# A four-layer hybrid model on one core: the first norm from the input's rows, inputs tile by tile, no weight part on GpSimd at the start, a shorter last norm, and unread products wherever TensorE's work thins out

## The chip, the cores and the metric

One core of a Trainium2 chip runs the whole kernel in one launch. The metric is the device time of that launch in microseconds. The engines are named as in the profile: PE (TensorE; PEld is its weight load), DVE (VectorE), ACT (ScalarE), POOL (GpSimd) and SP (SyncE, which issues most DMAs).

## The reference, cut to what matters

One sequence of 512 tokens, width 1024, float32, goes through four layers. Each has a token mixer and a SwiGLU feed-forward block of 2816 hidden columns, each ahead of it a norm, each added back to the residual. The mixers are, in turn, RWKV-7 (a recurrence with 16 heads of 64), attention over a window of 128 with a sink, a spatial gating unit and gated linear attention.

```python
def rmsnorm(x, g):
    xf = x.astype(jnp.float32)
    y = xf * lax.rsqrt(jnp.mean(jnp.square(xf), -1, keepdims=True) + NORM_EPS)
    return (y * g).astype(x.dtype)

# for each layer i:
#   x = x + mixer_i(rmsnorm(x, norm_mix[i]))
#   x = x + swiglu(rmsnorm(x, norm_ffn[i]), ffn_w_in[i], ffn_w_out[i])
# out = rmsnorm(x, norm_final)
```

## The kernel before

**Arithmetic.** A float32 operand is split into a high part (`whi`, a rounding on ACT) and a low part (`wlo`, a subtraction on DVE), both of a fast matmul type, and a product is made of three: high by high, high by low, low by high (`mm3`). `weights` loads a tile of 128x1024 (`wraw`) with a DMA from SP and splits it; with `pool` set, POOL does the subtraction. The feed-forward blocks make the products of a 2x2 blocking with seven multiplications in place of eight.

**Order.** The program isn't issued as it is written. Every operation is recorded with its dependences and a price (`price`), and `run` then issues one instruction at a time: of those that are free, the one that can start first by a model of the engines' times, which `now` keeps. So the order on each engine follows modelled times, not measured ones. All engine instructions leave from one line of `record`, and have that line in the profile: L233. Groups are therefore told apart by the names of their tiles.

**Unread products.** Before `run` issues a PE instruction that by the model starts at `s`, `keep_warm` looks at the gap since PE's last: if it is at least `GAP` = 450 ns, it is filled with products of a 128x128 identity by itself, into a PSUM bank that nobody reads. They are recorded as `ps<-ident` from L448. `count` adds up the columns that PE works off in each `TICK` of 3413 ns of the model, from which `run` guesses whether the clock is up.

**The start.** The residual lies in eight tiles `h` of 128 features x 512 tokens. They are loaded from `x_t`, the input with its axes exchanged. ACT squares the eight tiles, DVE adds them (7 additions), PE turns the sum (4 transposes, `ps<-ident,slot`) so that a reduction gives the mean square of each token (`ms`), `rsqrt` takes nine small steps to the reciprocal root (`rcol`), PE spreads it over the partitions (4 transposes, `ps<-ident,rcol`), DVE copies that out of the bank (`slot<-ps`), and the tiles are scaled one by one. Then comes the first product, of the mixer's key projection: eight steps `k`, each with a weight tile `rw_w_k` and 24 products `ps<-slot,whi` and `ps<-slot,wlo`.

**The first mixer** ends with the recurrence. Per group of heads it inverts triangular 64x64 blocks (`mt`, `iv`, `pr`, with copies between PE, DVE and ACT at each step), and then runs a chain over the chunks: `ps<-st,ident` and `ps<-st,qk` wait for the state, `ps<-vu,tok` for a copy by ACT. The out-projection is `ps<-et,rk`.

**The second mixer**, attention, makes scores for the heads of a group (`ps<-slot` of 128x256), exponentials and sums on ACT and DVE, and scaled rows on POOL; then PE turns the probabilities (`ps<-ident,slot`) and multiplies. Projections that don't depend on them (`ps<-whi,slot`, `ps<-wlo,slot`) may lie between.

**The last norm.** `finish` gathers the squares of each half of a row block and multiplies it by the norm's row `g` as it becomes ready; `store` scales each half (the left on DVE, the right on ACT) into a new tile, and sends out eight tiles of 128x512.

## Time and profile before

| | us |
|---|---|
| three timed runs, median (lowest to highest) | 2604.38 (2601.57 to 2606.51) |
| profiled execution, time | 2596.65 |
| its span | 2595.0 |
| its mean granted clock of PE | 0.994 |
| busy: PE, DVE, ACT, POOL | 2517.9, 1802.4, 1314.1, 377.6 |

Times in the views are microseconds from the start of the span. A row of a timeline gives the start, the length, the engine, the line, the operation, its output and inputs by their names, the shapes and the count of records, and in brackets the idle time ahead of it and what ended that. A row of a group gives the busy time, the mean of one record in ns, and the idle time of the engine ahead of such instructions with what ended most of it. Some float32 instructions of PE leave two records each; the unread products do.

### The profile page before, as it was taken

Reading aid. Unit: us, or ns where it says so; the run is one execution under the profiler, and the core shown is the slowest. Engines: PE = TensorE matmul, PEld = TensorE weight load, DVE = VectorE, ACT = ScalarE, POOL = GpSimd, SP = SyncE. Lnnn points to the kernel's source line nnn. Section 1 sums busy time; section 2 is a strip of 40 time slices with the busy share of each in tenths; the row PEclk is TensorE's granted clock in tenths of the full one; section 3 lists DMA queues with packets and bytes.
Section 4 is the critical chain, followed back from the end, with each engine's and each line's share of the span. In section 5 each row is a group of like instructions: output and inputs, shape, how many; then the busy total and the mean of one; then the engine's idle time right before and its main releaser. Section 6 shows DMA issues by size and latency. Waiting matters only on the chain.

```text
span 2595.0 us, 37573 instructions
## 1 busy us (share of the span) xinstructions
PE 2517.9 (97%) x14378; PEld 2052.6 (79%) x14378; DVE 1802.4 (69%) x2804; ACT 1314.1 (51%) x2156; POOL 377.6 (15%) x521
## 2 busy tenths in 40 slices
PE   9999898999999989999999999999999999999998
PEld 8577777997888756988787888888878777888886
DVE  8685875487778863787776655577868634577868
ACT  4544454465646455656464333565556523565555
POOL 1000111022112232121221000012111000121111
PEclk9999999999999999999999999999999999999999
DMA  3220001489898412898985232389887221489885
GB/s 128 62 75 10 10 4 59 120 195 225 214 225 176 129 49 49 179 211 225 213 218 146 90 98 83 82 216 228 208 213 187 84 81 57 98 219 226 221 199 117
DMA packets 126004, 365.20 MB, mean 141 GB/s; under 512 B 13296, under 2 KB 19952, under 8 KB 125824
## 3 DMA queue, kind: packets, MB, share of 16 engines
q0 software_dynamic: 41472, 138.43, 29.8%
q1 hardware_dynamic: 84352, 224.37, 26.9%
q8 instruction: 113, 1.85, 0.3%
q14 instruction: 67, 0.55, 0.1%
HBM read 358.29 MB, written 2.10 MB: 139 GB/s over the span
## 4 chain that ended last, share of the span: by engine, by line
PE 47%; DMA 5%; issue 5%; DVE 4%; ACT 3%; POOL 0%; SPq 0%; ACTq 0%; POOLq 0%; DVEq 0%
PE ps L233 47%; DMA wraw<-ffn_w_b 3%; DVE slot L233 2%; ACT slot L233 2%; DMA wraw<-ffn_o_a 2%; DVE wlo L233 1%; ACT whi L233 1%; DMA wraw<-ffn_w_a 1%; DVE h L233 0%; POOL wraw L233 0%; DVE mx L233 0%; DMA slot<-slot 0%; SPq L233 0%; DVE left L233 0%; ACT left L233 0%
## 5 line engine op out<-in xcount | busy, mean ns | idle before, releaser
L233 PE MATMUL ps<-whi,slot 128*128 128x512 f32 (+1 forms) x5072 | 1557.7, 384 | 17.8 <-DVE slot L233 9.3
L233 PEld LDWEIGHTS ps<-whi,slot 128*128 128x128 f32 x5072 | 943.7, 188 | 199.5 <-issue 21.4
L233 DVE TENSOR_TENSOR wlo<-wraw,whi 128x1024 fp32r<-128x1024 f32 (+2 forms) x628 | 720.2, 1153 | 398.8 <-ACT whi L233 396.4
L233 ACT CAST whi<-wraw 128x1024 fp32r<-128x1024 f32 (+3 forms) x632 | 625.1, 993 | 732.2 <-PE ps L233 554.7
L233 PE MATMUL ps<-wlo,slot 128*128 128x512 f32 (+1 forms) x2536 | 969.1, 383 | 1.9 <-DVE wlo L233 1.7
L233 PEld LDWEIGHTS ps<-wlo,slot 128*128 128x128 f32 x2536 | 476.9, 188 | 86.1 <-DVE wlo L233 6.2
L233 PE MATMUL ps<-slot,whi 128*128 128x512 f32 (+2 forms) x864 | 275.8, 397 | 0.1
L233 DVE TENSOR_TENSOR slot<-ps,slot 128x512 f32<-128x512 f32 (+2 forms) x287 | 155.0, 566 | 91.0 <-PE ps L233 61.7
L233 PEld LDWEIGHTS ps<-slot,whi 128*128 128x128 f32 (+2 forms) x864 | 157.2, 185 | 48.3 <-issue 6.6
L233 POOL DMA_DIRECT2D wraw<-ffn_w_a x128 | 109.1, 853 | 512.5 <-DVE wlo L233 375.7
L233 PE MATMUL ps<-slot,wlo 128*128 128x512 f32 (+2 forms) x432 | 169.5, 393 | 0.8 <-DVE wlo L233 0.8
L233 POOL DMA_DIRECT2D wraw<-ffn_w_b x64 | 54.7, 859 | 772.7 <-DMA wraw<-ffn_w_b 517.8
L233 DVE TENSOR_TENSOR slot<-left,slot 128x512 fp32r<-128x512 f32 (+1 forms) x214 | 137.5, 661 | 34.3 <-ACT slot L233 28.8
L233 DVE TENSOR_TENSOR h<-h,ps 128x512 f32<-128x512 f32 x192 | 127.1, 683 | 29.8 <-PE ps L233 28.4
L233 ACT CAST slot<-left 128x512 fp32r<-128x512 f32 (+1 forms) x214 | 123.8, 598 | 34.3 <-PE ps L233 26.4
L233 PEld LDWEIGHTS ps<-ident,slot 128*128 128x128 f32 (+1 forms) x676 | 69.2, 141 | 41.9 <-POOL slot L233 14.4
L233 ACT COPY slot<-ps 128x512 f32<-128x512 f32 (+1 forms) x137 | 75.2, 563 | 50.8 <-PE ps L233 49.2
L233 PE MATMUL ps<-ident,slot 128*128 128x128 f32 (+1 forms) x676 | 89.4, 268 | 11.4 <-POOL slot L233 9.0
L233 PEld LDWEIGHTS ps<-slot,wlo 128*128 128x128 f32 (+2 forms) x432 | 79.6, 184 | 21.3 <-issue 3.3
L233 POOL DMA_DIRECT2D wraw<-ffn_o_a x64 | 54.5, 852 | 278.6 <-DVE wlo L233 204.9
L233 ACT COPY left<-ps 128x512 f32<-128x512 f32 x100 | 50.5, 555 | 54.7 <-PE ps L233 54.7
L233 DVE TENSOR_TENSOR slot<-slot 128x512 fp32r<-128x512 f32 (+9 forms) x93 | 62.0, 672 | 15.8 <-ACT slot L233 14.6
(278 smaller groups left out, 2267.3 us busy)
## 6 DMA issues: line engine op xcount, KB each, us to landing
wraw<-ffn_w_a SPq DMA_DIRECT2D x128, 512.0 KB, 6.5
wraw<-ffn_w_a POOLq DMA_DIRECT2D x128, 512.0 KB, 6.1
wraw<-ffn_o_a SPq DMA_DIRECT2D x64, 512.0 KB, 5.0
wraw<-ffn_o_a POOLq DMA_DIRECT2D x64, 512.0 KB, 8.0
wraw<-ffn_w_b SPq DMA_DIRECT2D x64, 384.0 KB, 3.3
wraw<-ffn_w_b POOLq DMA_DIRECT2D x64, 384.0 KB, 6.2
wraw<-ffn_o_b SPq DMA_DIRECT2D x16, 512.0 KB, 4.3
wraw<-ffn_o_b POOLq DMA_DIRECT2D x16, 512.0 KB, 7.7
```

The source lines that it names most:

```text
L233: op = self.add(eng.name, lambda: getattr(eng.target, what)(*map(real, args), **{k: real(a) for k, a in kw.items()}), *self.price(eng.name ...
```

## The change

Four things, and all of them through the same recorder:

1. **First norm.** `token_squares` loads the input's rows `x` as eight tiles of 128 tokens x 512; six are squared with their sums on ACT, the last two go through DVE's statistics instructions, and the mean square of each token is there without a transpose. The tiles of `x_t` are loaded one by one within the loop over `k`, between the weight tiles. ACT, not DVE, copies the spread root out of the bank, and step `k` = 0 reads the bank itself (`near`).
2. **No weight part on POOL.** The first four subtractions of `rw_w_k` go to DVE like the others.
3. **Last norm.** The left half isn't multiplied by `g` ahead of time; `store` does that and the scaling in one instruction, both halves are scaled in place, and 4 transfers of 128x1024 take the place of 8.
4. **A guard.** `ahead_of_cold`: before a PE instruction is issued, the columns in the last `TICK` up to that instruction's modelled end are summed (`recent`). If they have once reached `DENSE` = 3500 and would now fall below it, an unread product goes ahead, and all is looked at again. It works for gaps of any length, shorter than `GAP` too.

```diff
@@ -194,7 +194,7 @@
     WINDOW, SLACK, SEM = 700, 200.0, 100.0
     FREE, GAP, TAIL, TURN = 4, 450.0, 150.0, 92.0
-    TICK, BUSY = 10240 / 3, 3350.0
+    TICK, BUSY, DENSE = 10240 / 3, 3350.0, 3500.0
     def __init__(self, tc):
         self.tc, self.ops, self.last = tc, [], None
@@ -202,6 +202,7 @@
         self.tensor, self.vector, self.scalar = Engine(self, "PE", nc.tensor), Engine(self, "DVE", nc.vector), Engine(self, "ACT", nc.scalar)
         self.gpsimd, self.sync = Engine(self, "POOL", nc.gpsimd), Engine(self, "SP", nc.sync)
         self.cold, self.warm, self.fills, self.form = 0.0, None, 0, (P, P, 0)
+        self.recent, self.armed = [], False
     def pool(self, name, bufs, **kw):
         return Pool(self, name, bufs, kw)
@@ -344,7 +345,7 @@
             s, i, op, e = best
             if e == "PE" and self.warm and op.ready > 0.0:
                 now["PE"] = self.keep_warm(now["PE"], s, work)
-                if now["PE"] > s:
+                if now["PE"] > s or self.ahead_of_cold(now, s, op, work):
                     continue
             avail[e].remove((i, op))
             if op.table and op.table != table and not (table and op.table in ALSO.get(table, ())):
@@ -412,7 +413,36 @@
             t += c
             now = t
+    def ahead_of_cold(self, now, s, op, work):
+        pool, call, first = self.warm
+        free = pool.slots["ps"].free
+        t, end = max(s, now["PE"]), s + op.cost
+        if not first.done or not free or min(free) + self.SEM > t:
+            return False
+        sum_ = op.columns
+        for b, e, c in reversed(self.recent):
+            if e <= end - self.TICK:
+                break
+            sum_ += c * (e - max(b, end - self.TICK)) / (e - b)
+        if sum_ >= self.DENSE:
+            self.armed = True
+            return False
+        if not self.armed:
+            return False
+        cost = 224.0 if work.get(int(t // self.TICK) - 1, 0.0) >= self.BUSY else 448.0
+        call()
+        self.fills += 1
+        self.form = P, P, 0
+        self.count(work, self.TICK, t, cost, 512.0)
+        now["PE"] = t + cost
+        return True
     def count(self, work, span, t, cost, columns):
+        self.recent.append((t, t + cost, columns))
+        if len(self.recent) > 400:
+            del self.recent[:200]
         n = int(t // span)
         part = min(1.0, ((n + 1) * span - t) / cost)
         work[n] = work.get(n, 0.0) + columns * part
@@ -598,8 +624,9 @@
             sq = self.slot()
             nc.scalar.activation(sq, self.h[b][:, c], AF.Square, accum_out=self.ss[:, 2 * b + nh:2 * b + nh + 1])
         if self.kind == 'final':
-            for b in bs:
-                nc.vector.tensor_mul(self.h[b][:, c], self.h[b][:, c], self.g[nh])
+            if nh:
+                for b in bs:
+                    nc.vector.tensor_mul(self.h[b][:, c], self.h[b][:, c], self.g[nh])
             return
         t = slice(half * 256, half * 256 + 256)
         for u in range(2):
@@ -673,25 +700,47 @@
         self.rsqrt(col, ms)
         return col
-    def rstd(self, acc=None):
+    def token_squares(self):
         nc = self.nc
-        if acc is None:
+        ss, ms = self.sm.tile([P, 2 * NB], F32, name="ss2"), self.sm.tile([P, NB], F32, name="ms")
+        st, mv = self.lay.tile([P, 2, 6], F32, name="xst"), self.lay.tile([P, 2], F32, name="xmv")
+        for j in range(2):
+            for b in range(NB):
+                x = self.slot()
+                nc.sync.dma_start(x, self.d['x'][b * P:(b + 1) * P, j * S:(j + 1) * S])
+                if b == NB - 1:
+                    nc.vector.bn_stats(st[:, j, :], x)
+                else:
+                    nc.scalar.activation(x, x, AF.Square, accum_out=ss[:, 2 * b + j:2 * b + j + 1])
+        nc.vector.bn_aggr(mv, st)
+        s2 = ss.rearrange("p (b n) -> p b n", b=NB)
+        l = NB - 1
+        nc.vector.scalar_tensor_tensor(ms[:, l:], mv[:, 0:1], mv[:, 0:1], mv[:, 1:2], op0=ALU.mult, op1=ALU.add)
+        nc.vector.tensor_scalar(ms[:, l:], ms[:, l:], EPS, None, op0=ALU.add)
+        nc.vector.tensor_add(ms[:, :l], s2[:, :l, 0], s2[:, :l, 1])
+        nc.vector.tensor_scalar(ms[:, :l], ms[:, :l], 1.0 / D, EPS, op0=ALU.mult, op1=ALU.add)
+        return ms
+    def rstd(self, ms=None):
+        nc = self.nc
+        if ms is None:
             col = self.rcol()
         else:
-            ms, col = [self.sm.tile([P, NB], F32, name=n) for n in ("ms", "rcol")]
-            ps = self.bank()
-            for b in range(NB):
-                nc.tensor.transpose(ps[:, b * P:(b + 1) * P], acc[:, b * P:(b + 1) * P], self.ident)
-            nc.vector.tensor_reduce(ms, self.blocks(ps), axis=AX.X, op=ALU.add)
-            nc.vector.tensor_scalar(ms, ms, 1.0 / D, EPS, op0=ALU.mult, op1=ALU.add)
+            col = self.sm.tile([P, NB], F32, name="rcol")
             self.rsqrt(col, ms)
         ps = self.bank()
         for b in range(NB):
             nc.tensor.transpose(ps[:, b * P:(b + 1) * P], col[:, b:b + 1].to_broadcast([P, P]), self.ident)
         bc = self.slot()
-        nc.vector.tensor_copy(bc, ps)
-        return col, bc
+        if ms is None:
+            nc.vector.tensor_copy(bc, ps)
+            return col, bc
+        nc.scalar.copy(bc, ps)
+        return ps, bc
     def operand(self):
         self.op = self.nx
@@ -933,18 +982,14 @@
         xq, tp = self.pool("xq", 8, tall), self.pool("tp", 3, tall)
         hn = self.h
+        ms = self.token_squares()
+        v = self.v = self.load_cols()
         nc.vector.memset(keep, 1.0)
         nc.vector.memset(self.blocks(keep, S // 64)[:, :, 0:1], 0.0)
         nc.vector.memset(sel, 0.0)
         nc.vector.memset(sel[:64, 14:15], 1.0)
         nc.vector.memset(sel[64:, 15:16], 1.0)
-        acc = self.slot()
-        for k in range(KT):
-            t = acc if k == 0 else tp.tile([P, S], F32, name="t")
-            nc.scalar.activation(t, hn[k], AF.Square)
-            if k:
-                nc.vector.tensor_add(acc, acc, t)
-        _, rbc = self.rstd(acc=acc)
+        near, rbc = self.rstd(ms)
         xx = []
         def mixed(c, k):
@@ -964,12 +1009,13 @@
         rf, kf = [[keepers.tile([P, S], F32, name="rk") for _ in range(KT)] for _ in range(2)]
         ps = [self.bank() for _ in range(KT)]
         for k in range(KT):
-            nc.vector.scalar_tensor_tensor(hn[k], hn[k], g(k), rbc, op0=ALU.mult, op1=ALU.mult)
+            nc.sync.dma_start(hn[k], d['x_t'][k * P:(k + 1) * P, :])
+            nc.vector.scalar_tensor_tensor(hn[k], hn[k], g(k), rbc if k else near, op0=ALU.mult, op1=ALU.mult)
             b = xq.tile([P, S], F32, name="xx")
             nc.vector.tensor_sub(b[:, 1:], hn[k][:, :S - 1], hn[k][:, 1:])
             nc.vector.tensor_scalar(b[:, 0:1], hn[k][:, 0:1], -1.0, None, op0=ALU.mult)
             xx.append(b)
-            hi, lo = self.weights(d['rw_w_k'][k * P:(k + 1) * P, :], 1, D, k < 4)
+            hi, lo = self.weights(d['rw_w_k'][k * P:(k + 1) * P, :], 1, D)
             x = mixed(2, k)
             for n in range(KT):
                 c = slice(n * P, (n + 1) * P)
@@ -1668,14 +1714,10 @@
             col = self.rcol(half * 2, half * 2 + 2)
             for j in range(2):
                 b = half * 2 + j
-                for nh in range(2):
-                    c = slice(nh * S, nh * S + S)
-                    o = self.slot()
-                    if nh:
-                        nc.scalar.activation(o, self.h[b][:, c], AF.Identity, scale=col[:, j:j + 1])
-                    else:
-                        nc.vector.tensor_scalar(o, self.h[b][:, c], col[:, j:j + 1], None, op0=ALU.mult)
-                    nc.sync.dma_start(self.d['out'][b * P:(b + 1) * P, c], o)
+                l, r = self.h[b][:, :S], self.h[b][:, S:]
+                nc.vector.scalar_tensor_tensor(l, l, col[:, j:j + 1], self.g[0], op0=ALU.mult, op1=ALU.mult)
+                nc.scalar.activation(r, r, AF.Identity, scale=col[:, j:j + 1])
+                nc.sync.dma_start(self.d['out'][b * P:(b + 1) * P, :], self.h[b])
 def consts():
@@ -1769,8 +1811,6 @@
 def trace(prog, d, es, stages):
     k = K(prog, d, es)
     k.h = k.eight()
-    k.load_x(k.h)
-    k.v = k.load_cols()
     g_mix = lambda i: (lambda j: k.v['norm_mix'](i * KT + j))
     g_ffn = lambda i: (lambda j: k.v['norm_ffn'](i * KT + j))
     for n, st in enumerate(stages):
```

Engine instructions now have L234, the unread products L478. By kind there are 262 unread products, 190 before: 67 up to the first product that counts (78 before), 164 from there to the end of the first mixer (90), 11 in attention (none), and 20 elsewhere (22).

**The start, on PE.** Before, the sum of squares is turned (`ps<-ident,slot`) between two runs of unread products:

```order
L448 MATMUL ps<-ident 128x128 x30
L233 MATMUL ps<-ident,vraw 128x128 x2
L448 MATMUL ps<-ident 128x128 x6
L233 MATMUL ps<-ident,slot 128x128 x4
L448 MATMUL ps<-ident 128x128 x19
L233 MATMUL ps<-ident,rcol 128x128 x4
L448 MATMUL ps<-ident 128x128 x23
L233 MATMUL ps<-slot,whi 128x512 x6
```

Now, up to the same first product:

```order
L478 MATMUL ps<-ident 128x128 x30
L234 MATMUL ps<-ident,vraw 128x128 x2
L478 MATMUL ps<-ident 128x128 x20
L234 MATMUL ps<-ident,rcol 128x128 x4
L478 MATMUL ps<-ident 128x128 x17
L234 MATMUL ps<-slot,whi 128x512 x8
```

The transposes of the sum are gone, and 37 unread products stand where 48 stood. On SP eight tiles of `x`, the two of `vecs` and then `x_t` and `rw_w_k` in turn take the place of eight tiles of `x_t`, `vecs` and five of `rw_w_k`. On DVE the first `wlo` stands ahead of the last step to `rcol`.

**The last inverse of the first mixer, on PE.** Its steps wait for copies of each other's results. Before, other groups' work lies between them, and no unread product:

```order
L233 MATMUL ps<-wu,iv 64x64 x5
L233 MATMUL ps<-mt 64x64 x16
L233 MATMUL ps<-wu,iv 64x64 x7
L233 MATMUL ps<-ident,mt 64x64 x16
L233 MATMUL ps<-vu,pr 64x64 x3
L233 MATMUL ps<-mt,pr 64x64 x16
L233 MATMUL ps<-vu,pr 64x64
L233 MATMUL ps<-wu,iv 64x64 x2
L233 MATMUL ps<-mt 64x64 x16
L233 MATMUL ps<-wu,iv 64x64
L233 MATMUL ps<-iv,mt 64x64 x24
```

Now:

```order
L478 MATMUL ps<-ident 128x128 x2
L234 MATMUL ps<-mt 64x64 x16
L478 MATMUL ps<-ident 128x128 x4
L234 MATMUL ps<-ident,mt 64x64 x16
L478 MATMUL ps<-ident 128x128 x3
L234 MATMUL ps<-mt,pr 64x64 x16
L478 MATMUL ps<-ident 128x128 x4
L234 MATMUL ps<-mt 64x64 x16
L234 MATMUL ps<-iv,mt 64x64 x7
L478 MATMUL ps<-ident 128x128 x4
L234 MATMUL ps<-iv,mt 64x64 x9
```

Unread products stand ahead of the same steps, and the chain's products (`wu,iv`, `vu,pr`) come after them. Behind this, in the last chain, 33 products of the out-projection `ps<-et,rk` stand between the chain's steps, where before 1 did.

**Attention, second group of heads, on PE.** `ps<-slot` are the scores, `whi` and `wlo` the out-projection of the group before, and `ps<-ident,slot` the first transposes of the probabilities. Before:

```order
L233 MATMUL ps<-slot 128x256 x9
L233 MATMUL ps<-whi,slot 128x512
L233 MATMUL ps<-wlo,slot 128x512
L233 MATMUL ps<-whi,slot 128x512 x2
L233 MATMUL ps<-wlo,slot 128x512
L233 MATMUL ps<-whi,slot 128x512 x2
L233 MATMUL ps<-wlo,slot 128x512
L233 MATMUL ps<-ident,slot 128x128 x2
L233 MATMUL ps<-whi,slot 128x512
```

Now the last rows of a run that is three times as long:

```order
L234 MATMUL ps<-whi,slot 128x512 x2
L234 MATMUL ps<-wlo,slot 128x512
L234 MATMUL ps<-whi,slot 128x512 x2
L234 MATMUL ps<-wlo,slot 128x512
L234 MATMUL ps<-whi,slot 128x512
L478 MATMUL ps<-ident 128x128 x3
L234 MATMUL ps<-ident,slot 128x128 x2
L234 MATMUL ps<-whi,slot 128x512
```

Between the scores and the transposes there are 24 products of the out-projection and 3 unread ones (8 and none before). In the first group of heads there are 33 for 11 at the same place. What moves ahead is missing from a later run. In the scores of each group stand 4 unread products. From the second feed-forward block on PE's order is that of before, up to two unread products in the tail that are gone.

More of the change, by code (lines that the diff above doesn't have):

```diff
@@ L940, in rwkv @@
         nc.vector.memset(sel[64:, 15:16], 1.0)
-        acc = self.slot()
-        for k in range(KT):
-            t = acc if k == 0 else tp.tile([P, S], F32, name="t")
-            nc.scalar.activation(t, hn[k], AF.Square)
-            if k:
-                nc.vector.tensor_add(acc, acc, t)
-        _, rbc = self.rstd(acc=acc)
+        near, rbc = self.rstd(ms)
         xx = []
```

4 lines of the change are left out of this document (1 added, 3 removed).

## The prediction

> **What bounds the kernel now.** I read the busy times of the engines first, then the chain of work that ended last, and then a table of busy time by stage.
>
> ```profile
> PE 2517.9 (97%) x14378; PEld 2052.6 (79%) x14378; DVE 1802.4 (69%) x2804; ACT 1314.1 (51%) x2156; POOL 377.6 (15%) x521
> PE 47%; DMA 5%; issue 5%; DVE 4%; ACT 3%; POOL 0%; SPq 0%; ACTq 0%; POOLq 0%; DVEq 0%
> ```
>
> TensorE is busy for 2517.9 us of 2595.0, so all idle time together is 77 us, and an edit can gain only in the stages where PE waits or where its clock is down. The table by stage says where these are (columns: length, then busy time and instructions of PE, its weight loads, DVE, ACT and POOL, the granted clock, the DMA share and GB/s).
>
> ```profile
> 0.00:24.36 24.36, 20.90 (x167) 20.58 (x167) 16.02 (x37) 9.04 (x12) 5.36 (x8) 1.00 0.60 205
> 24.36:195.00 170.64, 167.03 (x796) 119.64 (x796) 133.83 (x222) 82.41 (x123) 6.93 (x13) 1.00 0.23 71
> 195.00:480.00 285.00, 263.94 (x3625) 219.79 (x3620) 185.53 (x386) 127.80 (x271) 43.56 (x147) 0.99 0.08 24
> 480.00:890.00 410.00, 405.21 (x2011) 343.12 (x2010) 315.63 (x436) 229.85 (x343) 82.45 (x87) 1.00 0.80 190
> 890.00:1005.00 115.00, 101.19 (x449) 60.55 (x448) 68.52 (x159) 62.70 (x209) 39.06 (x37) 0.96 0.23 66
> 1005.00:2575.00 1570.00, 1551.62 (x7314) 1282.92 (x7313) 1069.72 (x1527) 795.72 (x1186) 200.22 (x229) 1.00 0.67 162
> 2575.00:2595.00 20.00, 8.05 (x36) 5.95 (x34) 13.13 (x41) 6.61 (x13) 0.00 (x0) 0.78 0.28 105
> ```
>
> Four stages have something to win: the first 24.36 us, in which PE does nothing but unread products; the recurrence of the first mixer (195 to 480), with 285.00 − 263.94 = 21.1 us idle; the attention of the second (890 to 1005), with 13.8 us idle at a clock of 0.96; and the last 20 us. The order of the instructions is the same in both kernels from the second feed-forward block to the tail, and there I change nothing.
>
> **The start.** The timeline from the first unread product to the first product that counts:
>
> ```profile
> 1.43 8.96 PE L448 MATMUL ps<-ident 128*128 128x128 f32 x60 [1.43 <-POOL ident L233]
> 7.42 2.67 ACT L233 ACTIVATE t<-h 128x512 f32<-128x512 f32 x4 [0.52 <-DMA h<-x_t]
> 10.22 0.38 PE L233 MATMUL ps<-ident,vraw 128*128 128x128 f32 x2
> 12.23 4.67 POOL L233 TENSOR_TENSOR wlo<-wraw,whi 128x1024 fp32r<-128x1024 f32 x2 [10.86 <-ACT whi L233]
> 13.04 0.69 DVE L233 TENSOR_REDUCE ms<-ps 128x4 f32<-128x512 f32 x1 [0.81 <-PE ps L233]
> 17.16 0.17 DVE L233 SCALAR_TENSOR_TENSOR rs_t<-ms,rs_t 128x4 f32<-128x4 f32 x1
> 17.36 0.16 DVE L233 SCALAR_TENSOR_TENSOR rcol<-rs_t,rcol 128x4 f32<-128x4 f32 x1
> 18.84 0.62 PE L233 MATMUL ps<-ident,rcol 128*128 128x128 f32 x4 [1.60 <-DVE rcol L233]
> 19.30 5.30 PE L448 MATMUL ps<-ident 128*128 128x128 f32 x46
> 19.50 0.69 DVE L233 COPY slot<-ps 128x512 f32<-128x512 f32 x1 [0.81 <-PE ps L233]
> 24.36 1.76 PE L233 MATMUL ps<-slot,whi 128*128 128x512 f32 x6
> L233 DVE TENSOR_TENSOR wlo<-wraw,whi 128x1024 fp32r<-128x1024 f32 (+2 forms) x628 | 720.2, 1153 | 398.8 <-ACT whi L233 396.4
> ```
>
> An unread product leaves two records, so 46 records are 23 products and one costs 5.30 / 23 = 0.23 us. On PE's side the new start is 30 products to 10.4, the two transposes of the vectors to 10.6, 20 products × 0.23 = 4.6 to 15.2, the transposes of rcol 0.62 to 15.8, and 17 × 0.23 = 3.9 to 19.7. On the data's side: the eight tiles of x stand first on SP, as those of x_t did, so the last square can begin about where a fifth tile's would, 7.42 + 3 × 0.67 = 9.4, and the last tile's statistics (one 128x512 pass of DVE, 0.69) end near 10.8. Then DVE has some 16 small steps at 17.36 − 17.16 = 0.2 us, 3.2 us, and one subtraction of a weight's low part, which now stands ahead of the last step of rcol: 1.15. That gives 15.2, so both sides meet at rcol near 15.2 to 15.8. From the transposes of rcol to the first product there were 24.36 − 18.84 = 5.5 us, of which the copy of 0.69 goes, since the first tile is scaled straight from the bank: 4.8. The first product comes at about 20.2, 4.2 us earlier. If the vectors, the first x_t and the first weight, which now stand behind 2 MB of x on SP, come late, rcol is held behind that subtraction and as little as 2 us is left; if the model's order binds at 19.7, it is 4.7. I take **−4.2**.
>
> The four subtractions that leave POOL took 4.67 / 2 = 2.33 us each there and take 1.15 on DVE, 4.6 us of new DVE work between the first product and the fifth tile. They lie beside 24 products per tile, of 0.23 us each: 5.5 us of PE per tile against some 4.2 of DVE (the subtraction, and four passes of 0.69 to 0.9). While that cover holds they cost nothing; without it, 4 × 1.15 = 4.6. One wait for a low part goes with them, of 0.78:
>
> ```profile
> 47.81 0.50 PE L233 MATMUL ps<-slot,wlo 128*128 128x512 f32 x1 [0.78 <-DVE wlo L233]
> ```
>
> With it the start is worth **−5** (−1 to −6).
>
> **The recurrence of the first mixer.** Here the guard puts in most: the count of unread products from 24 us to the end of this mixer goes from 90 to 164, 74 more. The groups of PE instructions that wait, and the row of the unread ones:
>
> ```profile
> L233 PE MATMUL ps<-vu,tok 128*128 128x128 f32 x112 | 20.5, 305 | 4.5 <-ACT vu L233 4.3
> L233 PE MATMUL ps<-et,rk 128*128 128x256 f32 x156 | 19.2, 282 | 0.0
> L448 PE MATMUL ps<-ident 128*128 128x128 f32 x126 | 16.9, 281 | 0.0
> L233 PE MATMUL ps<-st,ident 128*128 128x128 f32 x96 | 16.7, 296 | 3.7 <-DVE st L233 3.6
> L233 PE MATMUL ps<-ident,mt 64*64 64x64 f32 x384 | 14.6, 229 | 3.9 <-DVE mt L233 3.8
> L233 PE MATMUL ps<-mt 64*64 64x64 f32 x384 | 13.8, 221 | 1.6 <-DVE mt L233 1.5
> L233 PE MATMUL ps<-mt,pr 64*64 64x64 f32 x256 | 9.2, 221 | 0.7 <-ACT mt L233 0.7
> L233 PE MATMUL ps<-iv,mt 64*64 64x64 f32 x192 | 7.9, 227 | 1.4 <-DVE iv L233 1.4
> ```
>
> One product costs 16.9 / 63 = 0.27 us here, so 74 are 19.9 us of PE. They cost nothing as far as they lie in waits: ahead of the inverse's steps there are 3.9 + 1.6 + 0.7 + 1.4 = 7.6 us of waits, and I let 2.4 more fall into the chain's; that hides 10 and leaves **+10** on the path. (All hidden: 0. None: +19.9.) Against that, 33 products of the out-projection, ps<-et,rk at 19.2 / 156 = 0.123 us, 4.1 us together, move from behind the last chain into its waits, of which there are 4.5 + 3.7 in all: **−3.5** (0 to −4.1). And the guard is to keep the clock up in that chain:
>
> ```profile
> 447.33 0.71 PE L233 MATMUL ps<-vu,tok 128*128 128x128 f32 x4 [1.45 <-ACT vu L233]
> 449.00:453.00 4.00, 3.82 (x19) 3.15 (x20) 0.98 (x3) 0.42 (x2) 2.09 (x11) 0.57 0.01 2
> ```
>
> In these 4 us the granted clock was 0.57, so at most 4 × 0.43 = 1.7 us was lost; I take **−1.2** (0 to −1.7). No wait ahead of it was longer than 1.45 us: what fell was the density, not one long gap. The Trainium skill, "TensorE: Matmul & The Clock Gate", section "Why this matters for your kernels", asks only for "No PE-idle gaps >~3µs between matmul bursts"; by that rule there is nothing to guard here and the 74 products buy no clock at all. The row at 449 speaks against the rule in this place; by the rule the term of −1.2 would be nought.
>
> The stage as a whole: +10 − 3.5 − 1.2 = **+5** (−6 to +16).
>
> **The attention of the second mixer.** The two long waits stand in the timeline, each ahead of the first transposes of the attention probabilities of a head group:
>
> ```profile
> 904.03 0.39 PE L233 MATMUL ps<-slot,wlo 128*128 128x512 f32 x1
> 904.26 0.62 PE L233 MATMUL ps<-slot,whi 128*128 128x512 f32 x2
> 909.12 1.01 PE L233 MATMUL ps<-ident,slot 128*128 128x128 f32 x4 [4.25 <-POOL slot L233]
> 970.50 0.69 PE L233 MATMUL ps<-ident,slot 128*128 128x128 f32 x2 [4.71 <-POOL slot L233]
> 909.00:913.00 4.00, 3.75 (x11) 1.70 (x11) 3.96 (x11) 2.55 (x10) 2.19 (x5) 0.65 0.00 0
> 970.00:975.00 5.00, 4.25 (x12) 2.03 (x12) 5.00 (x13) 5.00 (x21) 2.19 (x5) 0.50 0.00 0
> ```
>
> What is put there is mostly real work, taken from a run that comes later: 22 more products of the projection in the first (33 for 11) and 16 more of the out-projection, with 3 unread ones, in the second (24 for 8). At 904.26 − 904.03 = 0.23 us each these are 5.1 us for a wait of 4.25, and 3.7 + 0.7 = 4.4 for one of 4.71. The later runs shrink by as much, so the waits are saved but for what the products run over: −3.4 and −3.7. (The eight unread products inside the scores fall into DVE's smaller waits, or cost 8 × 0.23 = 1.8.) The two windows at half clock lose at most 4 × 0.35 + 5 × 0.50 = 3.9 us; half of that, 1.9, since part of it is waiting anyway. Sum **−9** (−2 to −12).
>
> **The tail.** The last multiplication by g is folded into the scaling, and out goes in 4 transfers for 8:
>
> ```profile
> 2584.19 0.69 DVE L233 TENSOR_TENSOR h<-h,slot 128x512 f32<-128x512 f32 x1
> 2588.80 0.88 DVE L233 TENSOR_SCALAR slot<-h,rcol 128x512 f32<-128x512 f32 x2
> ```
>
> Four passes of 0.69 leave DVE, of which at most one lies in the last 11 us, since the right half's multiplications were and stay the last. The left half's scaling gets its second tensor and goes from 0.44 to about 0.69, and a transfer waits for both halves of a row block. Gain of 0.7, loss of 0.5 and some issue time less: **−0.3** (−1 to +1).
>
> **The sum** is −5 + 5 − 9 − 0.3 = −9.3, on the profiled execution's 2596.65 us: 2587.3. The three timed runs have their median at 2604.38, 7.7 us above that execution, so it is from the median that I subtract: **2595.0 us**. A measurement of this kernel can tell some 0.2% from no change, 5.2 us: faster is below 2599.2, slower above 2609.6.
>
> **Rivals.**
>
> *The guard is on the path (slower).* In the first mixer every product that the guard puts in stands ahead of an instruction that was about to start; where the order's model waits longer than the chip, it delays PE for its full 0.27 us. If nothing is hidden, no clock is won and the out-projection moves in vain, that stage is 74 × 0.27 = 19.9 us longer, and the sum −5 + 19.9 − 9 − 0.3 = +5.6: 2610. It decides once this stage is over some 19 us longer. For it: PE is 93% busy there, and its waits, 21.1 us, are hardly more than what is put in. Against it: 15 us of these waits stand at just the steps ahead of which products now lie.
>
> *The waits of attention move (no change).* The probabilities of a head group come through a chain of ACT, DVE and POOL; if its end, not its start, sets the stage, PE waits as long at the next group, and −9 becomes −2: −2.3 in sum, 2602. For it: in the window at 970 DVE and ACT are busy for 5.00 of 5.00. Against it: over the stage ACT is busy for 62.7 and DVE for 68.5 of 115.
>
> *Everything is hidden (better).* The 74 products lie wholly in waits: −5 − 4.7 − 9 − 0.3 = −19, 2585. Against it: 19.9 us of products and 4.1 of moved work into 21.1 of waits.
>
> **How the numbers follow.** The forecast gets 0.55, the slower rival 0.15, the moved waits 0.20, the better one 0.10. The range leaves out the far half of the slower and a part of the better case, 2584 to 2608. Faster takes the better case and all but a tenth of the forecast's: 0.62; slower is its rival and what is left of the start's late loads: 0.17; the rest, 0.21, is within.
>
> **What would show it.** Right: the first product that counts near 20.2; the waits of 4.25 and 4.71 below 1.5 and no half clock at either, nor in the last chain of the first mixer; that mixer's recurrence longer by about 5 us, with ps<-et,rk between steps of its chain; the tail as it was. Wrong: a recurrence longer by over 16 us, a wait for wlo at every tile of the first projection, an attention stage that is still 113 us long, or a clock that falls at other places instead. A wait that comes up anew beyond 1005 us, where the order stands still, would make the sum wrong by something I haven't priced.

## The result and the profile after

Over 20 runs each, the changed kernel takes 2609.01 us (median; 2602.41 to 2615.66) and the kernel before 2599.97 (2591.21 to 2608.75): a ratio of 1.0033, interval 1.0023 to 1.0042. It is slower, by about 9 us. The two profiled executions differ by 12.3 us in span (2607.3 and 2595.0). Below are the two stages that decide it, first of before, then of after together with the page's busy times. Each stage lies between the same two instructions of PE in both kernels, called its landmarks: for the recurrence the first `ps<-slot,pa` and the first `ps<-whi,rk`, for attention a `ps<-slot,wlo` ahead of it and a `ps<-wlo,slot` behind it, with the same instructions between them, unread products left out. The columns are those of the prediction's table by stage.

```profile
193.91:500.32 306.41, 285.36 (x3837) 241.21 (x3834) 192.46 (x398) 133.08 (x278) 45.46 (x149) 0.99 0.12 38
860.43:1007.12 146.69, 132.88 (x592) 86.74 (x591) 89.32 (x191) 74.07 (x223) 46.93 (x43) 0.97 0.21 59
```

```profile
PE 2551.3 (98%) x14518; PEld 2077.8 (80%) x14518; DVE 1795.0 (69%) x2801; ACT 1313.8 (50%) x2161; POOL 368.2 (14%) x517
...
190.22:518.63 328.41, 316.99 (x3984) 265.71 (x3981) 192.16 (x398) 133.06 (x278) 43.64 (x149) 0.99 0.12 35
880.05:1021.07 141.02, 136.92 (x615) 92.13 (x613) 89.79 (x191) 73.63 (x223) 48.15 (x43) 0.96 0.24 66
288.00:292.00 4.00, 4.00 (x43) 3.21 (x39) 3.25 (x5) 2.64 (x5) 0.50 (x2) 0.50 0.00 0
920.00:924.00 4.00, 3.94 (x19) 3.07 (x20) 2.46 (x7) 0.00 (x0) 0.00 (x0) 0.50 1.02 352
```

PE is busier by 33 us and idle for 21 us less. By place, after against before: the start −3.7, the recurrence 328.41 − 306.41 = **+22.0**, the feed-forward block behind it +1.3, attention 141.02 − 146.69 = **−5.7**, and all the rest, where the order stands, −1.7, which sum to 12.3. That last stretch is no result: over the runs below it takes 1579.0 to 1588.1 us. The lengths between landmarks repeat better: four executions with before's order and its unread products have a recurrence of 306.3 to 308.2 us.

The start came as worked out. The first product that counts begins at 19.90 (24.36 before), with rcol held by the subtraction as the order had it:

```profile
13.45 1.23 DVE L234 TENSOR_TENSOR wlo<-wraw,whi 128x1024 fp32r<-128x1024 f32 x1
14.27 1.04 ACT L234 CAST whi<-wraw 128x1024 fp32r<-128x1024 f32 x1 [0.93 <-DMA wraw<-rw_w_k]
14.60 0.15 DVE L234 SCALAR_TENSOR_TENSOR rcol<-rs_t,rcol 128x4 f32<-128x4 f32 x1
...
15.70 0.60 PE L234 MATMUL ps<-ident,rcol 128*128 128x128 f32 x4
16.14 3.96 PE L478 MATMUL ps<-ident 128*128 128x128 f32 x34
...
19.90 1.42 PE L234 MATMUL ps<-slot,whi 128*128 128x512 f32 x5
```

The recurrence, by groups of PE instructions (the window 191 to 498.3 here holds what 195 to 480 held before):

```profile
L478 PE MATMUL ps<-ident 128*128 128x128 f32 x270 | 45.5, 296 | 0.9
L234 PE MATMUL ps<-et,rk 128*128 128x256 f32 x161 | 22.1, 287 | 0.0
L234 PE MATMUL ps<-vu,tok 128*128 128x128 f32 x112 | 19.7, 298 | 1.5 <-ACT vu L234 1.4
L234 PE MATMUL ps<-st,ident 128*128 128x128 f32 x96 | 16.9, 295 | 1.8 <-DVE st L234 1.8
L234 PE MATMUL ps<-ident,mt 64*64 64x64 f32 x384 | 15.8, 227 | 1.8 <-DVE mt L234 1.6
L234 PE MATMUL ps<-mt 64*64 64x64 f32 x384 | 14.1, 221 | 0.3 <-DVE mt L234 0.2
L234 PE MATMUL ps<-mt,pr 64*64 64x64 f32 x256 | 11.4, 234 | 0.1
L234 PE MATMUL ps<-iv,mt 64*64 64x64 f32 x192 | 10.6, 231 | 0.6 <-DVE iv L234 0.6
```

The waits did shrink: in the chain (`vu,tok` and `st,ident`) from 4.5 and 3.7 to 1.5 and 1.8, in the inverse (the last four rows) from 3.9, 1.6, 0.7 and 1.4 to 1.8, 0.3, 0.1 and 0.6. But the unread products went from 126 records and 16.9 us to 270 and 45.5: 72 products more took 28.6 us, 0.40 each. In the last inverse it looks like this:

```profile
447.64 1.15 PE L234 MATMUL ps<-mt,pr 64*64 64x64 f32 x32
448.71 2.13 PE L478 MATMUL ps<-ident 128*128 128x128 f32 x8
449.26 0.30 PEld L478 LDWEIGHTS ps<-ident 128*128 128x128 f32 x2 [0.25 <-PE ps L478]
450.77 1.08 PE L234 MATMUL ps<-mt 64*64 64x64 f32 x29
```

Between the landmarks the same groups of before and of after are these:

```profile
L448 PE MATMUL ps<-ident 128*128 128x128 f32 x170 | 22.0, 279 | 0.0
```

```profile
L478 PE MATMUL ps<-ident 128*128 128x128 f32 x314 | 50.5, 293 | 0.9
```

In the fence on the inverse, four products (8 records) take 2.13 us, 0.53 each, at a granted clock of 1.00; in the start 17 took 3.96, 0.23 each. The row of the weight load shows most of the difference: from the second product on, the load waits 0.25 us for the product before. Between the landmarks that occurs 15 times, 3.7 us in all, and not once in the kernel before. The order's model counts 0.224 for a product, or 0.448 where it takes the clock to be down.

In attention the wait ahead of the probabilities' transposes is gone; products of the projection stand there now and, last, three unread ones (the timeline, and the group of unread products in the window 909.7 to 1019):

```profile
989.96 0.39 PE L234 MATMUL ps<-whi,slot 128*128 128x512 f32 x1
990.19 0.83 PE L478 MATMUL ps<-ident 128*128 128x128 f32 x6
990.86 0.38 PE L234 MATMUL ps<-ident,slot 128*128 128x128 f32 x2
```

```profile
L478 PE MATMUL ps<-ident 128*128 128x128 f32 x22 | 5.7, 360 | 1.7 <-DVE slot L234 1.3
```

### The profile page after: what moved, and what is told of

Read it like the earlier page. It is cut to its first block, busy times and chain, and to the rows that moved or that the text cites. A ratio compares the mean times of both kernels' runs of the same rounds, so it can differ in the third digit from the quotient of the medians.

```text
span 2607.3 us, 37842 instructions
## 1 busy us (share of the span) xinstructions
PE 2551.3 (98%) x14518; PEld 2077.8 (80%) x14518; DVE 1795.0 (69%) x2801; ACT 1313.8 (50%) x2161; POOL 368.2 (14%) x517
## 4 chain that ended last, share of the span: by engine, by line
PE 49%; DMA 5%; DVE 4%; issue 4%; ACT 3%; POOL 1%; SPq 0%; DVEq 0%; POOLq 0%; ACTq 0%
PE ps L234 49%; DMA wraw<-ffn_w_b 2%; DVE slot L234 2%; DMA wraw<-ffn_o_a 2%; ACT slot L234 1%; DVE wlo L234 1%; ACT whi L234 1%; POOL wraw L234 1%; DMA wraw<-ffn_w_a 0%; DVE h L234 0%; DVE mx L234 0%; PE ps L478 0%; DMA wraw<-sg_w_v 0%; DMA slot<-slot 0%; DVE left L234 0%
## 5 line engine op out<-in xcount | busy, mean ns | idle before, releaser
L234 PE MATMUL ps<-whi,slot 128*128 128x512 f32 (+1 forms) x5072 | 1557.5, 384 | 17.6 <-DVE h L234 7.9
L234 PEld LDWEIGHTS ps<-whi,slot 128*128 128x128 f32 x5072 | 941.9, 188 | 201.2 <-issue 21.9
L234 DVE TENSOR_TENSOR wlo<-wraw,whi 128x1024 fp32r<-128x1024 f32 (+2 forms) x632 | 726.3, 1155 | 403.9 <-ACT whi L234 401.5
L234 ACT CAST whi<-wraw 128x1024 fp32r<-128x1024 f32 (+3 forms) x632 | 625.4, 993 | 731.3 <-PE ps L234 554.8
L234 PE MATMUL ps<-wlo,slot 128*128 128x512 f32 (+1 forms) x2536 | 967.5, 382 | 1.3 <-DVE wlo L234 1.2
L234 PEld LDWEIGHTS ps<-wlo,slot 128*128 128x128 f32 x2536 | 476.1, 188 | 85.5 <-DVE wlo L234 5.0
L234 PE MATMUL ps<-slot,whi 128*128 128x512 f32 (+2 forms) x864 | 275.1, 396 | 0.4 <-DVE slot L234 0.3
L234 DVE TENSOR_TENSOR slot<-ps,slot 128x512 f32<-128x512 f32 (+2 forms) x287 | 154.9, 566 | 68.5 <-PE ps L234 50.7
L234 PEld LDWEIGHTS ps<-slot,whi 128*128 128x128 f32 (+2 forms) x864 | 156.9, 184 | 49.0 <-DVE slot L234 6.9
L234 POOL DMA_DIRECT2D wraw<-ffn_w_a x128 | 109.4, 855 | 511.5 <-DVE wlo L234 399.6
L234 PE MATMUL ps<-slot,wlo 128*128 128x512 f32 (+2 forms) x432 | 169.5, 393 | 0.0
L234 POOL DMA_DIRECT2D wraw<-ffn_w_b x64 | 54.8, 865 | 766.3 <-DMA wraw<-ffn_w_b 494.1
L234 DVE TENSOR_TENSOR slot<-left,slot 128x512 fp32r<-128x512 f32 (+1 forms) x214 | 137.7, 662 | 34.8 <-ACT slot L234 29.3
L234 DVE TENSOR_TENSOR h<-h,ps 128x512 f32<-128x512 f32 x192 | 127.2, 683 | 30.4 <-PE ps L234 28.9
L234 ACT CAST slot<-left 128x512 fp32r<-128x512 f32 (+1 forms) x214 | 123.8, 599 | 32.9 <-PE ps L234 26.4
L234 ACT COPY slot<-ps 128x512 f32<-128x512 f32 (+1 forms) x138 | 75.7, 565 | 59.6 <-PE ps L234 53.3
L234 PEld LDWEIGHTS ps<-slot,wlo 128*128 128x128 f32 (+2 forms) x432 | 79.5, 184 | 20.2 <-issue 3.3
L234 POOL DMA_DIRECT2D wraw<-ffn_o_a x64 | 54.6, 854 | 275.8 <-DVE wlo L234 161.3
L234 PEld LDWEIGHTS ps<-ident,slot 128*128 128x128 f32 (+2 forms) x672 | 67.9, 139 | 29.3 <-issue 8.3
L234 PE MATMUL ps<-ident,slot 128*128 128x128 f32 (+2 forms) x672 | 87.4, 264 | 1.9 <-DVE slot L234 1.7
L478 PE MATMUL ps<-ident 128*128 128x128 f32 x524 | 84.6, 297 | 4.0 <-POOL ident L234 1.4
L478 PEld LDWEIGHTS ps<-ident 128*128 128x128 f32 x524 | 71.6, 200 | 13.9 <-PE ps L478 5.7
```

Of the source, the lines that this page charges most:

```text
L234: op = self.add(eng.name, lambda: getattr(eng.target, what)(*map(real, args), **{k: real(a) for k, a in kw.items()}), *self.price(eng.name ...
L478: self.nc.tensor.target.matmul(self.ps.tile_pool.tile([P, S], F32, name="ps")[:, :P], self.ident.real(), self.ident.real(), start=True, st ...
```

## The experiments

All ratios are to runs of the kernel before on the same chip, with 95% intervals. "Recurrence" and "attention" are the lengths between the landmarks above (before: 306.4 and 146.7 us), each from the one profiled execution of its version.

### Which part costs: the parts alone

**The change without the guard:**

```diff
-    TICK, BUSY, DENSE = 10240 / 3, 3350.0, 3500.0
+    TICK, BUSY, DENSE = 10240 / 3, 3350.0, 0.0
```

> The changed kernel with DENSE = 0, so that the guard never puts anything in; first norm, weight parts, loads and last norm as changed. Theory A (the guard's products in the first mixer's recurrence stand on PE's path, 22 us there by the two traces; the start gains 5.6): 5.6 us under the kernel before, ratio 0.998, recurrence as long as before. Rival B (the input loads or the new subtractions on DVE cost something further on, the guard is innocent): no faster than before, ratio 1.000 to 1.003.

Measured: 1.0019 (1.0008 to 1.0031). Theory A missed. The start is gained (−5.1 us at the landmark), attention is as before (146.5), and the recurrence is 320.3 long, 13.9 more, though it holds fewer unread products than before (x136 in place of x170 records). PE is idle in it for 29.4 us, where before has 21.1, and busy for 5.6 us more. It also has more half clock, a granted clock of 0.50:

```profile
188.83:509.16 320.33, 290.94 (x3804) 243.22 (x3800) 192.94 (x398) 135.13 (x280) 44.31 (x149) 0.96 0.12 36
...
376.00:384.00 8.00, 8.00 (x45) 5.82 (x45) 4.17 (x8) 0.57 (x1) 1.18 (x2) 0.50 0.01 2
436.00:448.00 12.00, 9.62 (x64) 7.94 (x66) 4.81 (x12) 4.42 (x11) 3.17 (x16) 0.57 0.08 23
```

The order of the recurrence had changed without the guard. **The kernel before with the guard alone** (the function and its call in `run`, nothing else):

```diff
-                if now["PE"] > s:
+                if now["PE"] > s or self.ahead_of_cold(now, s, op, work):
```

> The kernel before with the guard alone. Theory A: the recurrence longer by some 22 us, attention shorter by some 5.7: 16 us over before, ratio 1.006. Rival B: near before, 1.000 or under, since attention's gain is left alone.

Measured: 1.0053 (1.0036 to 1.0069), recurrence +21.9, attention −4.8: as theory A had it.

**The guard off in the first mixer, on elsewhere:**

```diff
-        if not self.armed:
+        if not self.armed or not op.tight:
```

This is the line that decides; `op.tight`, set elsewhere, is false for what the first mixer records.

> The changed kernel with the guard switched off for the instructions of the first mixer and on for all others. Theory A: start 5.6 and attention 5.7 are both gained, nothing is lost: 11 us under before, ratio 0.996. Rival C (attention's gain is only there because the stage starts later or with other loads in flight): as no_guard, 0.998.

Measured: 1.0024 (1.0011 to 1.0037). It misses twice. The recurrence is 320.8, as without the guard. And attention is 145.7, only 1.0 under before: with the guard on there and 15 unread products, PE's idle time fell from 13.8 to 6.1, but its busy time rose from 132.9 to 139.7. So attention's gain does not come with the guard in every order; a version below has it in another:

```profile
869.82:1015.55 145.73, 139.68 (x622) 94.21 (x621) 90.10 (x191) 73.72 (x223) 47.76 (x43) 0.95 0.23 64
```

**The guard's order without its products:**

```diff
         cost = 224.0 if work.get(int(t // self.TICK) - 1, 0.0) >= self.BUSY else 448.0
-        call()
```

> The changed kernel's order, instruction for instruction, but the 51 products that the guard itself put in are not issued (the model still counts their time, so that the order and the 211 products of the older rule stay). Theory A (the products' own time, 0.34 to 0.4 us each, is what is lost): some 51 x 0.34 = 17 us under the changed kernel, 8 under before, ratio 0.997. Rival D (the moved order costs: out-projection between the chain's steps, and other steps out of their best places, so that PE waits where the products were): within 5 us of the changed kernel, ratio 1.002 to 1.003, with the products' places idle.

Measured: 0.9961 (0.9945 to 0.9976), 0.72% below the changed kernel. This is the plainest result of the study: the order of the instructions that count is the same, and 51 products taken out turn a loss into a gain. The recurrence goes from 328.4 to 316.1 with 41 of them gone, 0.30 us each, and attention from 141.0 to 138.6.

```profile
189.81:505.86 316.05, 299.46 (x3902) 253.59 (x3899) 192.17 (x398) 132.21 (x278) 43.45 (x149) 0.97 0.13 37
866.76:1005.38 138.62, 133.87 (x599) 90.14 (x597) 89.52 (x191) 73.60 (x223) 47.78 (x43) 0.95 0.24 67
```

The clock over the recurrence fell from 0.99 to 0.97, and it was still quicker. Rival D allowed 5 us of gain over the changed kernel, and there are some 18, so most of it falls. But 316.1 is still 9.7 over before's recurrence: something of the changed order is left, and the versions without any product, below, put a number on it.

### What the new start did to the order

The order follows modelled times, and the unread products follow a grid of fixed 3413 ns ticks. The new start shifts all later work in the model, against that grid. To test whether this alone gives another order (a draw, from here on), the model's time began elsewhere:

```diff
-        now = {e: 0.0 for e in ("PE", "DVE", "ACT", "POOL", "SP", "")}
+        now = {e: 1508.149 for e in ("PE", "DVE", "ACT", "POOL", "SP", "")}
```

With 1508.149 ns and no guard, PE's order from the first product to the tail is the order of before.

> The changed kernel without the guard, and with the model's time begun at 1508.149 ns instead of 0, so that its first counted product has the modelled time that it had before. By that the order on PE is that of the kernel before from the first product to the tail, unread products included; first norm, loads, weight parts and last norm are as changed. Theory E (without the guard the new start lost time because the earlier modelled times drew another order of the recurrence, with deeper clock dips): the order of before brings it back, 5.6 us under before, ratio 0.998. Rival B (the new loads or DVE's subtractions cost later): as the version without the guard, 1.000 to 1.003.

Measured: 0.9982 (0.9971 to 0.9993). Recurrence 308.2, attention 147.3, as theory E had it. Of the start's 5.6 us only 4 are there, since this order has 72 unread products ahead of the first that counts, not 67, which then begins at 21.42. The same, with the guard on outside the first mixer:

> As phase_start, with the guard on for all instructions outside the first mixer; on PE the order then differs from before in the start, in attention and in the tail alone. Theory E: start 5.6 and attention 5.7 add up, 11 us under before, ratio 0.996. Rival C (attention's gain belongs to another recurrence): as phase_start.

Measured: 0.9955 (0.9942 to 0.9969); recurrence 306.3, attention 140.5. So the change's gains are real, start and attention add up in this order, and they had been paid away in the recurrence. The falls of the clock aren't fixed by the order alone: in the recurrence it is down near 282 us in the execution above and near 445 us in this one, in the same order.

```profile
189.70:496.03 306.33, 285.25 (x3837) 241.20 (x3834) 192.40 (x398) 132.98 (x278) 44.31 (x149) 0.99 0.12 38
855.70:996.21 140.51, 136.17 (x619) 91.11 (x617) 88.66 (x191) 73.94 (x223) 47.78 (x43) 0.98 0.23 64
```

**The kernel before, begun at 500 ns**, no other edit:

> The kernel before with nothing but the model's time begun at 500 ns instead of 0: same instructions but for 170 unread products where there were 190, order of the projections' ends, the recurrence and attention drawn anew. Theory E: slower, by something like the 14 us that the recurrence lost in the version without the guard, since the order of before was a good draw; ratio 1.003 to 1.008. Rival F (the order's draw moves little on the chip; what cost was the work in the start): 1.000, within 0.002.

Measured: 1.0047 (1.0032 to 1.0061), with +13.9 us in the recurrence. A number that computes nothing costs more than the whole change. PE's idle time there is 5.2 us longer and its busy time 8.7, and half clock shows again:

```profile
364.00:384.00 20.00, 15.74 (x94) 9.12 (x92) 14.49 (x27) 10.65 (x18) 4.61 (x16) 0.72 0.02 8
```

Is there a better draw? Of 120 beginnings, 6625 ns has the earliest modelled end without the guard.

> Without the guard, the model's time begun at 6625 ns: of 120 beginnings the one whose modelled end is the earliest, 14.9 us before that of the version with the order of before (which measured 0.9982). So far, without the guard, modelled and measured differences agreed within a few us (500 ns in the kernel before: 13.7 us modelled, 13 measured). Theory E says a better draw is worth its modelled gain, less 1 us for four more products in the start: ratio 0.993. Rival M (the order of before was the best that the chip has; the model's gain is in clock that the chip doesn't lose): no better than 0.998.

Measured: 0.9965 (0.9950 to 0.9980), between the two: theory E asked for 0.005 under the 0.9982 of the order of before, and there are 0.0017, with intervals that overlap. Its recurrence is 312.2 long, 4 more than that of the order of before, and it wins in attention, 138.3. The same draw with the guard outside the first mixer:

> The same draw with the guard on outside the first mixer. Modelled 5.1 us before the version with the order of before and the guard there (0.9955). Theory E: 0.9935. If the gains of the draw and of attention add up whole (15 and 6 us), 0.990; rival M: 0.9955 or above.

Measured: 0.9988 (0.9977 to 1.0000): a miss for both. The recurrence is 312.0 and attention 143.1; with ten unread products more there, PE's busy time rose from 132.9 to 138.8 and its idle time fell from 5.4 to 4.3 only. So the model's end is a poor guide: of three differences it forecast one (500 ns) came out, one at a third of its size, and one with the wrong sign.

### What a product costs

**Smaller products:** where the guard stands next to 64-row instructions (30 of 51), it issues a product of 64x64 by 64x64 (`small`, whose definition isn't shown).

```diff
-        call()
+        (self.small if self.form[0] == 64 else call)()
```

> The changed kernel's order and count of unread products, but where the guard puts one next to 64-row instructions (30 of its 51) it is a product of 64x64 by 64x64 in place of 128x128. Theory G (a guard's product is dear, 0.36 us, because PE turns from the 64-row shape to the 128-row shape and back): 30 x 0.13 = 4 us or more under the changed kernel, ratio to before about 1.0015. Rival H (it is dear because it stands before an instruction that was ready, whatever its shape): as the changed kernel, 1.0033.

Measured: 1.0015 (1.0004 to 1.0026). Recurrence 325.2 for 328.4: 3.2 us, 0.11 per product. So the shape is some of the price, as theory G says. It is a net figure: with the smaller products the clock over the recurrence was 0.97 for 0.99, so the shape alone may be worth more than 0.11.

**No unread product behind the start**, in the changed kernel's order. The guard's call is left out as above, and now that in `keep_warm`, too; the last two versions below have the same edit to `keep_warm`:

```diff
-            call()
+            if t < 24000.0:
+                call()
```

> The changed kernel's order once more, with no unread product at all behind the first product that counts: neither the guard's 51 nor the older rule's 144. Theory I (the older rule's products lie in waits and hold the clock): slower than the version without the guard's 51 by 5 to 20 us, that is 0.998 to 1.004 of the kernel before, with half-clock windows where it had none. Rival J (the clock is cheap, products only stand in the way): faster still than 0.996, by up to 144 x 0.1 = 14 us, 0.991.

Measured: 0.9950 (0.9930 to 0.9969). Rival J, for the sign: 144 more products gone, and not slower than with them (0.9961). The recurrence is now 308.6, 2.1 over before, at a clock of 0.96.

```profile
189.50:498.05 308.55, 273.75 (x3671) 227.29 (x3667) 188.79 (x394) 130.63 (x276) 43.14 (x149) 0.96 0.12 36
859.00:995.37 136.37, 129.73 (x592) 86.48 (x591) 89.45 (x191) 73.54 (x223) 47.79 (x43) 0.99 0.24 68
```

```profile
414.12 1.98 PE L234 MATMUL ps<-ident,mt 64*64 64x64 f32 x32 [4.39 <-DVE mt L234]
416.02 0.47 PE L234 MATMUL ps<-ident,qk 128*128 128x128 f32 x1
416.42 1.97 PE L234 MATMUL ps<-mt,pr 64*64 64x64 f32 x32
...
419.28 1.45 PE L234 MATMUL ps<-mt 64*64 64x64 f32 x32
```

The second fence shows what the products are for, and what it is worth. After a wait of 4.39 us, in which the changed kernel issues 20 products, the next 32 records take 1.98 us where they take 1.15 in the changed kernel. The clock's fall is real, but it costs 0.8 us in each of two steps and 0.3 in a third.

**The version with attention's gain, less the guard's 13 products:**

> The version with the order of before up to attention and the guard outside the first mixer (0.9955), but the 13 products that its guard puts in are not issued: only the moved real work is left of the guard. Theory K (attention's gain is the moved work alone): 13 x 0.25 = 3 us less, ratio 0.994 to 0.9955. Rival L (the products hold the clock there and are part of the gain): slower than with them, 0.997 or above, with longer half-clock windows in attention.

Measured: 0.9943 (0.9930 to 0.9956). Theory K: attention is 140.6 long without the 13 products and 140.5 with them, so in this order the whole gain is the moved work. The two ratios' intervals overlap, and the step from 0.9955 isn't shown by itself.

```profile
857.53:998.09 140.56, 134.98 (x592) 90.15 (x591) 89.41 (x191) 74.01 (x223) 47.27 (x43) 0.94 0.23 64
```

**The kernel before without its 112 unread products behind the start:**

> The kernel before, order kept, without the 112 unread products behind the first product that counts. Theory N (an unread product behind the start costs more than its clock is worth, in any order): faster, by up to the 0.08 us each that the older rule's products cost in the guard's order, 112 x 0.08 = 9 us at most, 0.9965 to 0.999. Rival I (they lie in waits and hold the clock, and only the guard's are in the way): slower, 1.001 to 1.005, with more windows at half clock in the recurrence.

Measured: 0.9971 (0.9957 to 0.9985), with the recurrence at 302.7 for 306.4, in the same order. Theory N: the older rule's products cost there too.

```profile
195.24:497.94 302.70, 269.21 (x3668) 223.75 (x3664) 190.22 (x397) 130.61 (x276) 45.61 (x149) 0.97 0.12 36
```

Beside the version without any product in the guard's order (308.6) this gives the order's own price: 308.6 − 302.7 = 5.9 us. With it the recurrence's +22.0 comes apart: 12.4 are the guard's 41 products (328.4 − 316.1), 5.9 the order, and 3.8 what the older rule's products cost more in that order than in that of before (316.1 − 308.6 = 7.5 against 306.4 − 302.7 = 3.7). Each is a difference of single executions.

**The quickest version less all of them:**

> New start, order of before up to attention, the guard's moved work in attention, and no unread product behind the start: the quickest version (0.9943) less its 110. Theory N: 0.991 to 0.9935. Rival I: 0.995 or above.

Measured: **0.9903** (0.9886 to 0.9921), 2578.57 us over five runs, where the kernel before took 2600.63 on that chip (the two medians alone give 0.9915). It beats both kernels: the new start, the order of before in the recurrence, the moved work in attention, and no unread product behind the start.

```profile
PE 2494.6 (97%) x14138; PEld 2025.3 (79%) x14138; DVE 1794.8 (70%) x2801; ACT 1313.0 (51%) x2161; POOL 368.8 (14%) x517
...
189.79:492.58 302.79, 269.36 (x3668) 223.93 (x3664) 190.14 (x397) 130.57 (x276) 44.65 (x149) 0.97 0.12 36
853.97:993.50 139.53, 134.09 (x593) 89.68 (x591) 88.54 (x191) 73.98 (x223) 47.81 (x43) 0.95 0.23 65
```

## Why the prediction was wrong, by its own steps

The prediction gave 2595 with a range of 2584 to 2608 and held a kernel slower by more than 0.2% for 0.17 likely. It came out slower. The slower rival, the guard on the path, is the one that happened, and its point of decision ("over some 19 us longer") was passed at 22.0. That its 2610 lies so near the 2609.01 measured is luck. It stood on a median of three runs, 2604.38, that was 4.4 us above that of twenty; the change was +9.0, not +5.6; and the rival had nothing hidden at 0.27 us a product, where waits of 9.6 us did go and the products cost more. Two figures of the working were off by themselves: the recurrence's range ended at +16, though its own worst case for the products was +19.9, and the better case with nine tenths of the forecast's 0.55 gives 0.60 for faster, not 0.62.

- **The start, −5:** right. First product at 19.90 for 20.2; −5.5 at 50 us with the wait for `wlo`. By the first landmark 1.8 of it had gone again; from 152 to 160 us the granted clock was 0.79, where before had 1.00.
- **The weight parts on DVE, nothing:** no wait for them appears in PE's rows; it wasn't tried alone.
- **The recurrence, +5:** this is the step that failed, +22.0 measured. The sum was 19.9 for the products, −13.5 for waits (10 filled by products, 3.5 by the out-projection) and −1.2 for the clock. Between the landmarks it was 28.5 for the products (from 22.0 to 50.5), −9.6 for waits (idle time from 21.1 to 11.4) and 3.1 more for the other groups: 22.0. *The price of a product* is the largest miss. It was taken as the mean of those already there, 0.27, and the new ones took 0.40: 28.6 us for 72. The runs show two parts of why, the turn to another shape (0.11 each where 30 were made smaller) and loads that wait for the product before (0.25 us, 15 times). *The waits* went less than forecast: those of the inverse from 7.6 to 2.8, where all were to go, and those of the chain from 8.2 to 3.3, where the products were to take 2.4 and the out-projection 3.5. The moved order gained nothing as a whole: without any product it takes 5.9 us more than that of before. *The clock's −1.2* wasn't gained: the fall at 449 is gone, but that at 285 grew to the 0.50 at 288 to 292.
- **Attention, −9:** −5.7. The idle time fell by 9.7, more than the 7.1 forecast for the two waits. What was missed is again what was put in, 5.7 us for 11 products (taking out the guard's share of them won 2.4), and the 1.9 for the clock, which was still at 0.50 at 920. That the gain comes at all depends on the order: with the guard off in the first mixer it was 1.0.
- **The tail, −0.3:** from 2571.9 in the one and 2584.1 in the other to the end it is 23.1 and 23.2 us. Nothing.
- **The rule of the Trainium skill** ("TensorE: Matmul & The Clock Gate", "Why this matters for your kernels"), no gap of over some 3 us in PE's work, was weighed against the guard. The traces agree that a gap of that length goes with a fall, as the row with 4.39 us shows; as a condition it is too narrow for this kernel, for the fall at 449 came after waits of 1.45 at most. That the recurrence had nothing to gain from the guard came out as by the rule all the same, but for another reason: the clock did fall, and filling cost more than that was worth.

What was in no term: that the change of the start draws another order of the recurrence. With the guard it is hidden under the guard's own redraw; without it, it cost 13.9 us.

Open: why a product's load waits for the product before it in the last inverse and not in the start. A PSUM bank that both write might be the reason; that was not tried. Nor is the clock's share of the 13.9 us settled: 8.3 of them are idle time of PE and 5.6 busy time, and how much half clock adds to each isn't shown.

## What to carry to other kernels

Count what is put into a wait at the price of the place where it goes, not at the mean of where such things stood, and count each wait once, whatever is to fill it. A filler that holds a clock pays only if the clock's loss, in us at that place, is more than the filler's own time on the path: take it out at the same order and look. Where a scheduler orders by modelled times, a change at the start re-deals all that follows; hold the order fixed, or the measurement is of the draw.

## What was unexpected of the hardware

Half clock is cheaper here than the products against it: the recurrence ran in 302.8 us at 0.97, with no unread product, and in 306.3 at 0.99 with the older rule's, in the same order. And PE's small float32 products don't have one price: 0.23 us in a long row, 0.40 on average of the 72 more that the recurrence got, many of them between steps of another shape.
